# Evictions ahead of later weight splits, products between the pieces of a chain's front, and a second chain begun inside the first one's end

## The chip, the cores and the metric

The kernel runs on one core of one Trainium2 chip. The metric is the device time of one execution in microseconds (us); the time given is the median of three runs. Three engines matter here: PE (TensorE, the matrix products), ACT (ScalarE) and DVE (VectorE). POOL (GpSimd) does a few additions, and SP (SyncE) issues the loads of the weights.

## What is computed

Two blocks of two layers each work on 256 tokens of width 1024, all in fp32. The first block (attention, Fourier and pooling mixers, mixture of experts) is not touched by the chain edits. The second block is, per layer:

```python
h = h + HALF * _swiglu(_rmsnorm(h, ffn1_norm[l]), ffn1_w_in[l], ffn1_w_out[l])
xn = _rmsnorm(h, mix_norm[l])
z = xn @ w_in[l]
z_rw = z_rw + shift_mu[l] * (_time_shift(z_rw) - z_rw)
r, k, v, xw, xa, xg = _split_cols(z_rw, RW_SPLITS)
y_a = _rwkv7_mixer(r, k, v, xw, xa, xg, ...)
y_b = _mlstm_mixer(mq, mk, mv, mo, mi, mf, ...)
u = jax.nn.sigmoid(g_a) * (y_a @ br_a[l]) + jax.nn.sigmoid(g_b) * (y_b @ br_b[l])
h = h + u @ w_out[l]
h = h + HALF * _swiglu(_rmsnorm(h, ffn2_norm[l]), ffn2_w_in[l], ffn2_w_out[l])
```

In the RWKV mixer the decay is built from `tanh(xw)`, a small product and a sigmoid; `a` is a sigmoid of a small product; `xg` goes through a sigmoid; the decay's running sum goes through exponentials; `kk` is `k * k_k`, divided by its norm. The recurrences of both mixers are worked out in chunks by triangular products.

## The kernel before

**Weights.** All weights lie in one stream in the order of use. SP loads them as tiles of 1536 KB into a ring. Every block of 128 x 1024 weights is one **job** of the class `Dense` (from L440). Its weights are split into a high and a low half: ACT copies the high half (`zh`, L451), DVE subtracts (`zl`, L452). There are three pairs of such halves. The products then run on PE, and an **eviction** (a closure in `evq`) takes the result out of PSUM.

**The pump.** `pump(k)` runs the next k jobs. Ahead of job n it writes out the splits of all jobs up to n + 2, then the products of job n, then a hook if the job has one, then the evictions of the jobs before n. `need(n)` (called by `upto`) pumps to job n and writes out the evictions of all jobs below n. The order in the text is a priority: the framework's planner puts an instruction of later text ahead on its engine where the earlier one isn't ready by its reckoning, so an engine's queue need not follow the text. Once planned, each queue runs in order.

**The mixer phase** (`mixer`) has 47 jobs: 4 for the mLSTM values, 15 for the RWKV inputs (`zr_job`, L1480 on for its eviction; list `ZR`: the three small inputs, k, r, v), 12 for the other mLSTM inputs, 16 for the gates (`zg_job`, whose eviction is a sigmoid on ACT, L1556). Then come 8 `br` jobs, which need the outputs of both chains, and 8 `w2` jobs, which need the evictions of the `br` jobs.

**The chains.** `rwkv` and `mlstm` are generators: a list of steps with a `yield` between two, and after each step the loop at the end of the phase pumps one job. `rwkv` has 22 yields; `mlstm` has 7. `START2 = 22` starts `mlstm` after the 22nd step, that is, just before the last piece of `rwkv`. The **front** of `rwkv` (L1630 to L1680) is: tanh and two sigmoids of the small inputs (L1632 to L1634), 8 small products with 8 sigmoids (L1645), 4 scans (L1649), sums, four exponentials (L1660 to L1664), squares of k (L1668), copies of k with a scale (L1670), the norm (`rows8`). Calls of `upto(ZN + ...)` in it say which jobs must be through. The **end** of `rwkv` is the output y (copies L500, sums L503), its mean (a product with a constant, written `ps<-t,c`), squares L1899, norm, gate, and the split of y_a. The end of `mlstm` is its norm, L2039, and the split of y_b (ACT L1294, DVE L503, written `p<-t`), which the `br` jobs wait for.

The other phases, in order: first block (two layers), then per layer of the second block a feed-forward phase (`ffn_phase`, 44 + 24 jobs; two jobs share one eviction), the mixer phase, a second feed-forward phase.

Of the kernel before, what the change touches and what calls it, by code (L numbers as in the profile page):

```python
# [9 lines left out]
AF = mybir.ActivationFunctionType  # L10
# [8 lines left out]
LATE = 0  # L19
QKO = [4, 5, 0, 1, 2, 3]  # L20
NSLOT = 16
START2 = 22
TILE_W = 3072
FF = 2816
NFF = FF // 128
# [408 lines left out]
class Dense:  # L434
# [21 lines left out]
    def flush(self, upto=None):  # L456
        while self.evq and (upto is None or self.evq[0][0] < upto):
            self.evq.pop(0)[1]()

    def pump(self, k=None):  # L460
        stop = len(self.jobs) if k is None else min(len(self.jobs), self.n + k)
        while self.n < stop:
            while self.split_n < min(len(self.jobs), self.n + self.ahead + 1):
                self.do_split(self.split_n)
                self.split_n += 1
            key, mm, ev = self.jobs[self.n]
            pair = self.split.pop(self.n)
            mm(*pair)
            self.whl.put(pair)
            if self.n in self.hooks:  # L470
                self.hooks.pop(self.n)()
            if not self.hold:
                self.flush(self.n + 1 - self.lag)
            if ev is not None:
                self.evq.append((self.n, ev))
            self.n += 1
        if k is None:
            self.flush()

# [780 lines left out]
def second(env):  # L1260
# [29 lines left out]
    def v4(t):  # L1290
        return t.rearrange("p (a b) -> p a b", b=256)
# [142 lines left out]
    def mixer(l, after):  # L1434
# [32 lines left out]
        def zr_job(b):  # L1467
            box = {}

            def run(wh, wl):  # L1470
                box["p"] = PS.get()
                block(box["p"][:, 0:256], wh, wl, Q2)

            def ev():
                p = box["p"]
                if b < 4:
                    dst = r[:, b * 4:b * 4 + 4]
                elif b < 12:
                    dst = g3(v4((k, v)[b // 4 - 1])[:, b % 4])
                else:  # L1480
                    dst = g3(lo_[:, b - 12])
                z = zs.get()
                acopy(z[:, 3:259], p[:, 0:256])
                d = sm.get()
                A.activation(d[:, 0:256], p[:, 0:256], AF.Copy, scale=mu1[:, b:b + 1])
                PS.put(p)
                V.scalar_tensor_tensor(dst, g3(z[:, 2:258]), K["mu", l][:, b:b + 1], g3(d[:, 0:256]), op0=ALU.mult, op1=ALU.add)
                sm.put(d)
                zs.put(z)
            return (("zr", l, b), run, ev)  # L1490
# [77 lines left out]
        def upto(n):  # L1568
            dn.need(n0 + n)
# [28 lines left out]
        def g3(ap):  # L1598
            return ap.rearrange("p (n c) -> p n c", c=64)
# [29 lines left out]

        def rwkv():  # L1630
            upto(ZN + 3)
            A.activation(lo_[0:64, 0], lo_[0:64, 0], AF.Tanh)  # L1632
            A.activation(lo_[:, 1], lo_[:, 1], AF.Sigmoid)
            A.activation(lo_[0:32, 2], lo_[0:32, 2], AF.Sigmoid)  # L1634
            upto(ZN + 5)
            sig, a = S.get(), S.get()
            for (lo, hi, dst, bias) in ((0, 64, sig, "rw_w0"), (64, 128, a, "rw_a0")):
                for half in range(2):
                    p = PS.get()
                    for n in range(2):  # L1640
                        hp = half * 2 + n
                        mm(p[:, n * 256:n * 256 + 256], lw[lo:hi, hp * 128:hp * 128 + 128], lo_[lo:hi, 0])
                    for n in range(2):
                        hp = half * 2 + n
                        A.activation(v4(dst)[:, hp], p[:, n * 256:n * 256 + 256], AF.Sigmoid, bias=K[bias, l][:, hp:hp + 1])  # L1645
                    PS.put(p)
            cum = S.get()
            for hp in range(4):
                V.tensor_tensor_scan(v4(cum)[:, hp], C["scan"], v4(sig)[:, hp], 0.0, op0=ALU.mult, op1=ALU.add)  # L1649

            f = rcol.get()
            f3 = f[:, 0:16].rearrange("p (h c) -> p h c", c=4)
# [5 lines left out]
            tt(V, g3(cum), g3(cum), ctr.rearrange("p (n o) -> p n o", o=1).to_broadcast([128, 16, 64]), ALU.subtract)  # L1658
            tt(V, sig, cum, sig, ALU.subtract)
            A.activation(f3[:, :, 0:3], f3[:, :, 0:3], AF.Exp, scale=-cexp)  # L1660
            A.activation(sig, sig, AF.Exp, scale=-cexp)
            em = S.get()
            A.activation(em, cum, AF.Exp, scale=cexp)
            A.activation(cum, cum, AF.Exp, scale=-cexp)  # L1664
            upto(ZN + 7)
            t = S.get()
            for hp in range(4):
                A.activation(v4(t)[:, hp], v4(k)[:, hp], AF.Square, scale=K["rw_k_k", l][:, hp:hp + 1])  # L1668
            for hp in range(4):
                A.activation(kk[:, hp * 4:hp * 4 + 4], g3(v4(k)[:, hp]), AF.Copy, scale=K["rw_k_k", l][:, hp:hp + 1])  # L1670
            upto(ZN + 8)
            nrm = yield from rows8(t, None, None, 1e-24)
            for hf in range(2):
                c = slice(hf * 8, hf * 8 + 8)
# [86 lines left out]
            LT, QB = tri(bm)  # L1761
            yield
            AT, QK = tri(km)
            yield
            vtok = turn(v, v)
            yield
            Gm = S.get()
# [120 lines left out]
                        tt(V, yv, g3(b_[2][w]), yv, ALU.add)  # L1888
            PS.put(*b_)
            S.put(vtok, U, QK, QB, SS)  # L1890
            yield
            b_ = two_banks()
            for hp in range(4):
                mm(b_[hp // 2][:, (hp % 2) * 256:(hp % 2) * 256 + 256], C["bmean"], v4(y)[:, hp])
# [151 lines left out]
        n = 0  # L2046
        while alive:
            for g in list(alive):
                try:
                    next(g)  # L2050
                except StopIteration:
                    alive.remove(g)
                dn.pump(1)
                n += 1
                if n == START2:
                    alive.append(g2)
# [152 lines left out]
```

## Time and profile before

| what | value |
|---|---|
| median of 3 runs | 2723.25 us (2720.39 to 2723.99) |
| profiled execution, device time | 2721.18 us |
| its span in the trace | 2719.4 us |
| mean granted PE clock | 0.974 |
| PE busy, share of the span | 91% |
| first block | up to 1378 us |
| first mixer / second mixer, as read below | 1583.4 to 1841.4 us / 2240.5 to 2499 us |

PE is busy for nine tenths of the span, so the reader looks for the places where it isn't, and asks what it waited for there. The granted clock of PE is 1.00 at its full speed (2.4 GHz) and 0.50 at its lower one (1.2 GHz): a stretch with a mean of 0.77 has lost 0.23 of its length. The trace counts time from the start of the span.

### The profile page before, as it was taken

What the parts mean: (1) busy time and instruction counts of PE and PEld (TensorE: products, weight loads), DVE (VectorE), ACT (ScalarE), POOL (GpSimd) and SP (SyncE); (2) the same over time, 40 slices, a digit from 0 to 9 for tenths busy, and PEclk for the clock granted to TensorE, in tenths of its full rate; (3) what the DMA queues carried; (4) which work ended last, traced back from release to release, by engine and by line L of the source; (5) the groups of instructions that cost most, each with busy time, mean ns of one, the idle gap of its engine ahead of it and who ended that gap; (6) DMA issues with size and microseconds to landing.
All of it is one profiled execution on the core that took longest, in us unless ns stands there. A gap on an engine that the chain in (4) does not pass through costs nothing.

```text
span 2719.4 us, 39461 instructions
## 1 busy us (share of the span) xinstructions
PE 2463.7 (91%) x16536; PEld 1713.8 (63%) x16536; DVE 1249.3 (46%) x2221; ACT 952.9 (35%) x1620; POOL 157.5 (6%) x185
## 2 busy tenths in 40 slices
PE   7998999999999865656689999999999999999998
PEld 4756443333366511111158889898888889989887
DVE  3544221111265300000057668557667677756765
ACT  3332100000043200000045574446556557454654
POOL 0100000000010000000011100011111100001111
PEclk9999999999999899899989999999999999999999
DMA  8372799999946699999965533234545543223553
GB/s 342 117 297 103 333 395 425 426 426 426 426 195 264 266 426 426 425 426 426 426 259 193 186 140 118 95 121 175 196 180 189 196 181 140 95 94 118 186 183 111
DMA packets 66915, 689.95 MB, mean 254 GB/s; under 512 B 7216, under 2 KB 9648, under 8 KB 11056
## 3 DMA queue, kind: packets, MB, share of 16 engines
q1 hardware_dynamic: 65584, 681.76, 62.6%
q0 software_dynamic: 720, 4.76, 0.4%
q8 instruction: 129, 2.11, 0.3%
q10 hardware_dynamic: 432, 0.91, 0.1%
q14 instruction: 50, 0.41, 0.0%
HBM read 686.35 MB, written 1.05 MB: 253 GB/s over the span
## 4 chain that ended last, share of the span: by engine, by line
PE 73%; DMA 20%; DVE 4%; ACT 2%; issue 1%; POOL 0%; SPq 0%; DVEq 0%; ACTq 0%; POOLq 0%
PE ps L492 71%; DMA xring<-in_w_dram 9%; DMA ring<-in_w_dram 7%; DMA mring<-in_w_dram 4%; PE ps L1736 1%; DVE zl L452 1%; ACT zh L451 1%; DVE t L503 0%; PE ps L892 0%; POOL sm L503 0%; DMA h<-in_cT_dram 0%; DVE sm L503 0%; DVE hl L1038 0%; DVE p L1339 0%; DVE t L1649 0%
## 5 line engine op out<-in xcount | busy, mean ns | idle before, releaser
L452 DVE TENSOR_TENSOR zl<-ring,zh 128x1024 fp32r<-128x1024 f32 (+1 forms) x398 | 480.0, 1207 | 287.6 <-ACT zh L451 287.2
L451 ACT ACTIVATE zh<-ring 128x1024 fp32r<-128x1024 f32 (+1 forms) x398 | 414.3, 1041 | 485.5 <-PE ps L492 385.6
L492 PE MATMUL ps<-p,zh 128*128 128x512 f32 (+1 forms) x1664 | 542.6, 378 | 11.9 <-ACT zh L451 5.7
L492 PE MATMUL ps<-p,zl 128*128 128x256 f32 x1536 | 433.4, 282 | 1.8 <-DVE zl L452 1.8
L492 PEld LDWEIGHTS ps<-p,zh 128*128 128x128 f32 x1664 | 307.1, 190 | 71.9 <-ACT zh L451 6.6
L492 PE MATMUL ps<-xring,m 128*64 128x512 f32 (+1 forms) x1280 | 296.7, 616 | 57.6 <-DMA xring<-in_w_dram 56.8
L492 PE MATMUL ps<-ring,m 128*64 128x512 f32 (+1 forms) x1288 | 298.1, 611 | 48.7 <-DMA ring<-in_w_dram 48.1
L492 PE MATMUL ps<-q,zh 128*128 128x256 f32 x1632 | 316.1, 293 | 7.5 <-ACT q L1294 2.9
L492 PEld LDWEIGHTS ps<-p,zl 128*128 128x128 f32 x1536 | 293.5, 191 | 2.5 <-DVE zl L452 2.3
L492 PEld LDWEIGHTS ps<-q,zh 128*128 128x128 f32 x1632 | 260.7, 196 | 17.9 <-ACT q L1294 4.4
L492 PE MATMUL ps<-act,zh 128*128 128x512 f32 x704 | 247.6, 393 | 0.0
L492 PEld LDWEIGHTS ps<-xring,m 128*64 128x64 f32 (+1 forms) x1280 | 86.1, 127 | 246.6 <-issue 140.6
L492 PE MATMUL ps<-q,zl 128*128 128x256 f32 x816 | 235.4, 289 | 2.9 <-DVE zl L452 1.5
L492 PEld LDWEIGHTS ps<-ring,m 128*64 128x64 f32 (+1 forms) x1288 | 88.0, 127 | 229.9 <-issue 136.0
L503 DVE TENSOR_TENSOR m<-ps,m 128x512 f32<-128x512 f32 x24 | 16.6, 692 | 447.2 <-PE ps L492 447.2
L492 PE MATMUL ps<-act,zl 128*128 128x256 f32 x704 | 199.6, 284 | 0.0
L492 PEld LDWEIGHTS ps<-q,zl 128*128 128x128 f32 x816 | 160.2, 196 | 1.9 <-DVE zl L452 1.9
L500 ACT ACTIVATE m<-ps 128x512 f32<-128x512 f32 x24 | 14.3, 598 | 419.7 <-PE ps L1190 284.9
L1202 DVE SCALAR_TENSOR_TENSOR h<-ps,mods,h 128x256 f32<-128x256 f32 x160 | 69.5, 480 | 187.4 <-PE ps L492 187.4
L492 PEld LDWEIGHTS ps<-act,zh 128*128 128x128 f32 x704 | 132.2, 188 | 30.2
L492 PE MATMUL ps<-mring,m 128*32 128x512 f32 x504 | 91.5, 659 | 59.4 <-DMA mring<-in_w_dram 59.4
L492 PEld LDWEIGHTS ps<-act,zl 128*128 128x128 f32 x704 | 132.4, 188 | 0.0
(323 smaller groups left out, 3053.3 us busy)
## 6 DMA issues: line engine op xcount, KB each, us to landing
ring<-in_w_dram SPq DMA_DIRECT2D x228, 1536.0 KB, 8.2
xring<-in_w_dram SPq DMA_DIRECT2D x129, 1536.0 KB, 15.9
mring<-in_w_dram SPq DMA_DIRECT2D x42, 1536.0 KB, 29.4
ring<-in_w_dram SPq DMA_DIRECT2D x31, 1408.0 KB, 5.9
ring<-in_w_dram SPq DMA_DIRECT2D x4, 1280.0 KB, 19.5
lora<-in_lora_dram POOLq DMA_DIRECT2D x2, 768.0 KB, 7.3
cf<-in_cf_dram POOLq DMA_DIRECT2D x1, 1392.5 KB, 12.4
h<-in_xT_dram SPq DMA_DIRECT2D x1, 1024.0 KB, 6.3
```

The source lines that it names most:

```text
L451: nc.scalar.activation(hi[:, :c], w, AF.Copy)
L452: nc.vector.tensor_tensor(lo[:, :c], w, hi[:, :c].bitcast(F32), op=ALU.subtract)
L492: PE.matmul(o, lhsT=lhsT, rhs=rhs, start=start, stop=stop, skip_group_check=True)
L500: A.activation(o, a, AF.Copy)
L503: e.tensor_tensor(o, a, b, op=op)
L1202: V.scalar_tensor_tensor(h[:, kb, c], p[:, c], mods[i][:, 5, kb, r:r + 1], h[:, kb, c], op0=ALU.mult, op1=ALU.add)
L1736: PE.transpose(b_[n // 4][:, (n % 4) * 128:(n % 4) * 128 + 128], src[:, n * 128:n * 128 + 128], ident)
```

## The change

`pump` now writes out the splits only up to job n + 1 ahead of job n, and that of job n + 2 behind the hook and the evictions that follow job n (new method `split_to`). In the eviction of `zr_job` the plain copy moves from ACT to DVE. In the front of `rwkv` the two sigmoids stand ahead of the tanh; the 8 small products go to four banks at once; six `upto` calls are spread between the pieces (one more job is asked for by the time of the norm); the sigmoid of the running sum's exponential follows a job; the scaled copies of k move from ACT to DVE. After the third step of `rwkv` no job is pumped (`yield 0`), after the step that builds y two are (`yield 2`). `mlstm` starts after step 19 instead of 22, and as long as `rwkv` lives, a step of `mlstm` pumps nothing.

```diff
--- before.py
+++ after.py
@@ -19,7 +19,7 @@
 LATE = 0
 QKO = [4, 5, 0, 1, 2, 3]
 NSLOT = 16
-START2 = 22
+START2 = 19
 TILE_W = 3072
 FF = 2816
 NFF = FF // 128
@@ -457,12 +457,15 @@
         while self.evq and (upto is None or self.evq[0][0] < upto):
             self.evq.pop(0)[1]()
 
+    def split_to(self, n):
+        while self.split_n < min(len(self.jobs), n):
+            self.do_split(self.split_n)
+            self.split_n += 1
+
     def pump(self, k=None):
         stop = len(self.jobs) if k is None else min(len(self.jobs), self.n + k)
         while self.n < stop:
-            while self.split_n < min(len(self.jobs), self.n + self.ahead + 1):
-                self.do_split(self.split_n)
-                self.split_n += 1
+            self.split_to(self.n + self.ahead)
             key, mm, ev = self.jobs[self.n]
             pair = self.split.pop(self.n)
             mm(*pair)
@@ -474,6 +477,7 @@
             if ev is not None:
                 self.evq.append((self.n, ev))
             self.n += 1
+            self.split_to(self.n + self.ahead)
         if k is None:
             self.flush()
 
@@ -1480,7 +1484,7 @@
                 else:
                     dst = g3(lo_[:, b - 12])
                 z = zs.get()
-                acopy(z[:, 3:259], p[:, 0:256])
+                V.tensor_copy(z[:, 3:259], p[:, 0:256])
                 d = sm.get()
                 A.activation(d[:, 0:256], p[:, 0:256], AF.Copy, scale=mu1[:, b:b + 1])
                 PS.put(p)
@@ -1629,24 +1633,26 @@
 
         def rwkv():
             upto(ZN + 3)
-            A.activation(lo_[0:64, 0], lo_[0:64, 0], AF.Tanh)
             A.activation(lo_[:, 1], lo_[:, 1], AF.Sigmoid)
             A.activation(lo_[0:32, 2], lo_[0:32, 2], AF.Sigmoid)
-            upto(ZN + 5)
+            A.activation(lo_[0:64, 0], lo_[0:64, 0], AF.Tanh)
+            upto(ZN + 4)
             sig, a = S.get(), S.get()
-            for (lo, hi, dst, bias) in ((0, 64, sig, "rw_w0"), (64, 128, a, "rw_a0")):
-                for half in range(2):
-                    p = PS.get()
-                    for n in range(2):
-                        hp = half * 2 + n
-                        mm(p[:, n * 256:n * 256 + 256], lw[lo:hi, hp * 128:hp * 128 + 128], lo_[lo:hi, 0])
-                    for n in range(2):
-                        hp = half * 2 + n
-                        A.activation(v4(dst)[:, hp], p[:, n * 256:n * 256 + 256], AF.Sigmoid, bias=K[bias, l][:, hp:hp + 1])
-                    PS.put(p)
+            up = [[PS.get(), PS.get()] for _ in range(2)]
+            for hp in range(4):
+                for m, (lo, hi) in enumerate(((0, 64), (64, 128))):
+                    mm(up[m][hp // 2][:, (hp % 2) * 256:(hp % 2) * 256 + 256], lw[lo:hi, hp * 128:hp * 128 + 128], lo_[lo:hi, 0])
+            for m, (dst, bias) in enumerate(((sig, "rw_w0"), (a, "rw_a0"))):
+                if m:
+                    upto(ZN + 5)
+                for hp in range(4):
+                    A.activation(v4(dst)[:, hp], up[m][hp // 2][:, (hp % 2) * 256:(hp % 2) * 256 + 256], AF.Sigmoid,
+                                 bias=K[bias, l][:, hp:hp + 1])
+                PS.put(*up[m])
             cum = S.get()
             for hp in range(4):
                 V.tensor_tensor_scan(v4(cum)[:, hp], C["scan"], v4(sig)[:, hp], 0.0, op0=ALU.mult, op1=ALU.add)
+            upto(ZN + 6)
 
             f = rcol.get()
             f3 = f[:, 0:16].rearrange("p (h c) -> p h c", c=4)
@@ -1658,17 +1664,18 @@
             tt(V, g3(cum), g3(cum), ctr.rearrange("p (n o) -> p n o", o=1).to_broadcast([128, 16, 64]), ALU.subtract)
             tt(V, sig, cum, sig, ALU.subtract)
             A.activation(f3[:, :, 0:3], f3[:, :, 0:3], AF.Exp, scale=-cexp)
-            A.activation(sig, sig, AF.Exp, scale=-cexp)
             em = S.get()
             A.activation(em, cum, AF.Exp, scale=cexp)
+            upto(ZN + 7)
+            A.activation(sig, sig, AF.Exp, scale=-cexp)
             A.activation(cum, cum, AF.Exp, scale=-cexp)
-            upto(ZN + 7)
+            upto(ZN + 8)
             t = S.get()
             for hp in range(4):
                 A.activation(v4(t)[:, hp], v4(k)[:, hp], AF.Square, scale=K["rw_k_k", l][:, hp:hp + 1])
             for hp in range(4):
-                A.activation(kk[:, hp * 4:hp * 4 + 4], g3(v4(k)[:, hp]), AF.Copy, scale=K["rw_k_k", l][:, hp:hp + 1])
-            upto(ZN + 8)
+                V.tensor_scalar(kk[:, hp * 4:hp * 4 + 4], g3(v4(k)[:, hp]), K["rw_k_k", l][:, hp:hp + 1], None, op0=ALU.mult)
+            upto(ZN + 9)
             nrm = yield from rows8(t, None, None, 1e-24)
             for hf in range(2):
                 c = slice(hf * 8, hf * 8 + 8)
@@ -1761,7 +1768,7 @@
             LT, QB = tri(bm)
             yield
             AT, QK = tri(km)
-            yield
+            yield 0
             vtok = turn(v, v)
             yield
             Gm = S.get()
@@ -1888,7 +1895,7 @@
                         tt(V, yv, g3(b_[2][w]), yv, ALU.add)
             PS.put(*b_)
             S.put(vtok, U, QK, QB, SS)
-            yield
+            yield 2
             b_ = two_banks()
             for hp in range(4):
                 mm(b_[hp // 2][:, (hp % 2) * 256:(hp % 2) * 256 + 256], C["bmean"], v4(y)[:, hp])
@@ -2046,11 +2053,12 @@
         n = 0
         while alive:
             for g in list(alive):
+                k_ = None
                 try:
-                    next(g)
+                    k_ = next(g)
                 except StopIteration:
                     alive.remove(g)
-                dn.pump(1)
+                dn.pump(0 if g is g2 and g1 in alive else 1 if k_ is None else k_)
                 n += 1
                 if n == START2:
                     alive.append(g2)
```

## Rows read from the trace of the kernel before

**Rows 1.** The page's busy time of PE, its share of the span, its instructions.

```profile
PE 2463.7 (91%) x16536; PEld 1713.8 (63%) x16536; DVE 1249.3 (46%) x2221; ACT 952.9 (35%) x1620; POOL 157.5 (6%) x185
```

**Rows 2.** The chain that ended last, share of the span by engine.

```profile
PE 73%; DMA 20%; DVE 4%; ACT 2%; issue 1%; POOL 0%; SPq 0%; DVEq 0%; ACTq 0%; POOLq 0%
```

**Rows 3.** Windows (length, busy time by engine, clock, DMA): feed-forward, both mixers.

```profile
1400.00:1583.00 183.00, 183.00 (x1042) 160.33 (x1041) 127.84 (x191) 105.09 (x180) 22.43 (x28) 1.00 0.52 188
...
1583.40:1841.40 258.00, 247.84 (x2998) 232.53 (x2996) 170.50 (x291) 140.12 (x221) 8.69 (x7) 0.97 0.30 111
2240.50:2499.00 258.50, 248.46 (x3006) 233.58 (x3004) 173.29 (x292) 142.93 (x226) 8.11 (x6) 0.97 0.30 107
```

**Rows 4.** Windows again, order PE, PEld, DVE, ACT, POOL: the mixer's front.

```profile
1599.50:1617.20 17.70, 15.87 (x122) 14.88 (x120) 11.75 (x17) 15.85 (x32) 0.00 (x0) 1.00 0.25 90
...
1612.40:1627.40 15.00, 12.94 (x88) 12.32 (x89) 5.72 (x12) 14.00 (x26) 0.00 (x0) 0.77 0.28 106
1627.50:1655.50 28.00, 28.00 (x308) 26.14 (x305) 27.87 (x43) 10.77 (x19) 0.00 (x0) 1.00 0.32 114
...
2268.00:2288.00 20.00, 18.15 (x129) 17.56 (x128) 9.43 (x18) 16.05 (x28) 0.00 (x0) 0.74 0.30 108
```

**Rows 5.** ACT in order of time, front (start, us, line, operation, tiles, shapes).

```profile
1595.52 1.28 ACT L1632 ACT_TABLE_LOAD   x1
...
1597.88 1.28 ACT L1633 ACT_TABLE_LOAD   x1
...
1608.90 1.28 ACT L1660 ACT_TABLE_LOAD   x1
1610.20 0.21 ACT L1660 ACTIVATE rc<-rc 128x12 f32<-128x12 f32 x1
...
1613.19 1.04 ACT L1664 ACTIVATE t<-t 128x1024 f32<-128x1024 f32 x1
1614.14 1.04 ACT L451 ACTIVATE zh<-ring 128x1024 fp32r<-128x1024 f32 x1
```

**Rows 6.** DVE groups by form (count, us, ns): first mixer, then 1627.5 to 1655.5.

```profile
L503 DVE TENSOR_TENSOR t<-ps,c 128x256 f32<-128x256 f32 x16 | 5.6, 413 | 0.0
L1739 DVE COPY t<-ps 128x512 f32<-128x512 f32 x8 | 5.5, 684 | 0.8 <-PE ps L1736 0.8
...
L1487 DVE SCALAR_TENSOR_TENSOR t<-zs,k,sm 128x256 f32<-128x256 f32 x4 | 1.9, 479 | 0.1
```

**Rows 7.** PE in time at `ps<-t,c`; PE's waits, 2400 to 2430.

```profile
1753.58 0.67 PE L492 MATMUL ps<-t,c 128*128 128x256 f32 x2 [1.79 <-DVE t L503]
...
PE ps L492 <- issue: 1.4, 1, 1.4
PE ps L492 <- DVE t L503: 0.9, 1, 0.9
```

**Rows 8.** Windows: the chains' ends, one job, the wait ahead of `br` and `w2`.

```profile
1744.00:1783.00 39.00, 36.82 (x417) 32.43 (x416) 21.96 (x39) 29.28 (x40) 0.59 (x1) 0.96 0.28 103
...
1787.99:1790.94 2.95, 2.95 (x27) 2.95 (x26) 1.78 (x3) 0.23 (x1) 0.00 (x0) 1.00 0.97 412
...
1808.00:1822.00 14.00, 10.91 (x78) 10.50 (x77) 8.44 (x15) 4.41 (x6) 0.72 (x1) 0.88 0.01 1
...
1834.00:1842.00 8.00, 5.96 (x43) 5.15 (x43) 6.26 (x13) 3.30 (x6) 1.22 (x1) 1.00 0.38 152
```

**Rows 9.** Feed-forward: ACT and DVE in time, and the 88 evictions' silu group.

```profile
1451.60 1.06 ACT L451 ACTIVATE zh<-ring 128x1024 fp32r<-128x1024 f32 x1 [1.12 <-issue]
...
1455.35 0.40 ACT L1294 ACTIVATE act<-sm 128x256 fp32r<-128x256 f32 x1
...
1457.15 1.06 ACT L451 ACTIVATE zh<-ring 128x1024 fp32r<-128x1024 f32 x1 [1.14 <-PE ps L492]
...
1452.69 1.23 DVE L452 TENSOR_TENSOR zl<-ring,zh 128x1024 fp32r<-128x1024 f32 x1 [0.41 <-ACT zh L451]
...
L1392 ACT ACTIVATE sm<-sm 128x256 f32<-128x256 f32 x88 | 36.0, 409 | 5.4 <-DVE sm L503 5.3
```

## What the change should do, worked out from these rows

> **What bounds the kernel now.** I read the page's busy times first: PE works 91% of the span [rows 1]. The chain that ended last says the same from the other side: 73% of it is PE, 20% loads of weights, ACT and DVE have 6% [rows 2]. The loads belong to the first block, which the chain edits don't reach. So the next view is busy time by stretch, for the parts that the change touches. A feed-forward phase has PE at 183.00 of 183.00 us: nothing is to be had there [rows 3]. The two mixers have 247.84 of 258.00 and 248.46 of 258.50: 10.2 and 10.0 us of idle PE, plus a mean clock of 0.97, which is 0.03 x 258 = 8 us in each [rows 3]. The number of products doesn't change, so some 36 us is all that a new order can win in the mixers, and the question is which of those holes it closes. They are few. The front of `rwkv`: PE is idle 15.00 - 12.94 = 2.06 us, and the clock of that stretch is 0.77, so 15 x 0.23 = 3.5 us more; in the second mixer 20.00 - 18.15 = 1.85 us and 20 x 0.26 = 5.2 us [rows 4]. The end of `rwkv`: PE waits 1.79 us for y; in the second mixer 1.4 + 0.9 = 2.3 us [rows 7]. The end of `mlstm`: 14.00 - 10.91 = 3.09 us idle, clock 0.88, so 14 x 0.12 = 1.7 us more, and the second mixer repeats both. Ahead of the `w2` jobs: 8.00 - 5.96 = 2.04 us, repeated too [rows 8].
>
> **The front.** Between 1599.5 and 1617.2 ACT is busy 15.85 of 17.70 us, DVE 11.75 [rows 4]. In the queue the split of the next weights (`zh`, 1614.14) stands right behind the exponentials (L1664 at 1613.19) [rows 5], and PE ran dry meanwhile. The change does two things there. It asks for single jobs between the pieces, so a split comes up before the exponentials and not behind them all. And it takes work off ACT: per mixer 15 plain copies and 4 scaled ones go to DVE. A DVE instruction of 128 x 256 from PSUM takes 0.41 us, and a copy of 128 x 512 takes what a difference of that size does, 0.68 [rows 6], so I price each at 0.41. In the front's 17.7 us that is some 4 + 4 of them: 3.3 us, which makes DVE's 11.75 into 15.1 of 17.7. It still fits. I take the idle time as closed but for 0.4 us a mixer (3.1 of 3.9 won). The low clock began only after the idle time, and in the next 28 us, with PE at 28.00 of 28.00, it is 1.00 [rows 4]; so with the hole most of the loss should go: 4.9 of 8.7. Together **8.0 us**, with bounds 0 and 12.6.
>
> The tanh now stands behind the sigmoids. Today a table load of 1.28 us stands ahead of the tanh and another ahead of the sigmoid [rows 5]. Its input is the first of the three to be ready, so a queue set by readiness keeps tanh first and both loads; the other way one load fewer or one more is ACT's 1.28 us a mixer, inside the bounds above. I take nothing. The Trainium skill (ScalarE: Activation LUTs, "Table sets: the hidden batching unit") lists tanh in the set of the sigmoid as well as in that of exp; by it, sigmoid first would save one load, and the sum would gain at most 2.6 us in two mixers; today's order with its two loads agrees with it, and no row here shows the other order.
>
> **DVE after the front.** From 1627.5 to 1655.5 DVE is busy 27.87 of 28.00 us [rows 4]: it paces the chain there, under a PE that is just as full. Seven evictions of `zr` jobs fall in this stretch (4 in the row, 3 more of that form that write r) [rows 6]. Seven copies of 0.41 are 2.9 us a mixer, 5.7 in two, on the path if PE has no other job, nothing if it has. I take about half, **-2.4 us**; bounds 0 and -5.7.
>
> **The end of `rwkv`.** `yield 2` puts a second job of 2.95 us [rows 8] where PE now waits 1.79 us for y (2.3 in the second mixer) [rows 7]. Its weights can be split by then, since three pairs exist. The job was due after step 3 before, next to the stretch where PE is at 28.00 of 28.00 [rows 4]. I take **3.6** of 4.1 us; bounds 0 and 4.1.
>
> **The end of `mlstm`.** Steps 1 to 3 of `mlstm` now run inside the last three pieces of `rwkv` and pump nothing. So of the 47 jobs the last three are pumped later: one after step 7, one after the end of the chain, one by the final pump, where before none was left after step 6. Two jobs, 5.9 us, stand against a hole of 3.09 us [rows 8]. That closes it with room: I take 5.6 of 6.2 us idle and half of the clock's 3.4, **7.3 us**; bounds 0 and 9.6. The price is paid inside: the overlapped stretch has two jobs fewer to hide behind. From 1744 to 1783 ACT is busy 29.28 of 39.00 us [rows 8]; without 5.9 us of that time and without two splits of 1.06 it would have 27.2 of 33.1.
>
> **Evictions ahead of splits.** In the feed-forward phases, where 88 evictions lie [rows 9], the split that begins at 1451.60 is done at 1453.9 (DVE 1452.69 + 1.23); it is used two jobs after it became possible, when the split two jobs on begins, 1457.15: 3.2 us of slack hide the edit [rows 9]. If the whole eviction went ahead of it (its last ACT copy ends at 1455.75, less the 1.06 us of the split that no longer stands in its way), the split would be done at 1454.7 + 1.06 + 1.23 = 1457.0, still just in time. I take 0; bound: 0.1 us x 88 = -9 us. Loads of weights that SP issues when a split is through move by the same fraction of a microsecond, in phases where the loads aren't late. Ahead of `w2` the evictions of the last `br` jobs come earlier, by at most the 2.04 us twice; I take **0.4 us**, bounds 0 and 4.1.
>
> **The sum.** 8.0 - 2.4 + 3.6 + 7.3 + 0.4 = 16.9 us. The profiled execution took 2721.18 us, 2 us below the median; there the sum gives 2704, and against the median 2723.25 it gives **2706 us**. All upper bounds together are 30.4 us, 2693.
>
> **Rivals.**
> (A) The front stays as it is, because DVE takes over as the bound: 15.1 of 17.7 us plus waits leaves little room, and the copies cost their full 5.7 - 0.9 us. Against it: DVE has 5.95 us free there today [rows 4]. Then 3.6 + 7.3 + 0.4 - 4.8 = 6.5 us: **2717**.
> (B) The change doesn't do what it says. Queues follow readiness and not the text, as the split copy of the eviction behind a later job's split in rows 9 shows (1455.35), and the overlap only shifts the holes: **2722**. Against it: the number of jobs after each step is fixed by data and banks, not by readiness.
> (C) Slower: table loads. In the overlap the gate evictions (sigmoid) meet exp, ln, square root of two chains instead of one, and each change of function set costs ACT a load of 1.28 us, after which it goes on at once (1608.90 + 1.28 to 1610.20) [rows 5]. ACT has 33.1 - 27.2 = 5.9 us free there, so it decides from five more loads a mixer on. With ten more, 12.8 us, ACT overruns by 6.9 us a mixer and the end's gains are lost: 13.8 - 8.0 + 2.4 = 8 us slower, **2731**. For it: today the stretch already alternates. Against it: fewer jobs in it mean fewer gate evictions. The Trainium skill (ScalarE: Activation LUTs, "What ACT_TABLE_LOAD costs") puts a change of set at about 2.66 us, the load and a drain as long again; the row here shows 1.28 and no drain. By the page three more loads would already decide, and ten would give some 2759.
>
> **How the numbers follow.** A measurement of this kernel can tell about 0.2%, 5.4 us. Forecast 0.62, A 0.20, B 0.09, C 0.09. A lies close to that limit, so I count 0.12 of it as faster and 0.08 as the same: faster 0.74, same 0.17, slower 0.09. The range runs from all upper bounds, 2692, to 2722, which takes in A and half of B; C is left out.
>
> **What would show it.** In the front: a `zh` of L451 between the sigmoids L1645 and the exponentials, idle PE under 1 us, clock near 1.00 over 15 us. At `ps<-t,c`: 48 products ahead of it, no wait. At the end: `q` jobs between the norm of `mlstm` and the `br` jobs, no wait of 2.5 us for the split of y_b. DVE's full stretch: its length against 28 us. Wrong would be: a PE wait for `zl` instead of `zh` in the front (A), the same holes at later places (B), over ten loads of tables at the ends (C), or idle PE in the feed-forward phases.

## The result, and the profile after

The changed kernel takes 2691.70 us (median; 2689.02 to 2692.10) where the kernel before, timed beside it, takes 2721.82. The ratio is 0.9888, with a 95% interval of 0.9871 to 0.9905: 30.5 us less, 25.9 to 35.1. The forecast was 2706 in 2692 to 2722: right in sign and in the places, too small by nearly half, and the median lies just below the low end of the range. The profiled execution has a span of 2689.8 us. After the change, the lines of the code lie 4 to 7 further down: L492 is now L496, L503 is L507, L1294 is L1298.

First the windows that answer [rows 3, 4, 8]. Columns: window, its length, then busy us (and instructions) of PE, PEld, DVE, ACT, POOL, then the clock, the DMA share, GB/s.

```profile
1400.00:1583.00 183.00, 183.00 (x1046) 160.49 (x1045) 127.74 (x190) 105.37 (x181) 22.38 (x28) 1.00 0.51 186
1588.00:1848.00 260.00, 258.03 (x3145) 245.13 (x3146) 191.67 (x326) 144.06 (x219) 10.50 (x13) 0.99 0.33 121
2245.60:2505.60 260.00, 258.03 (x3126) 244.14 (x3125) 191.64 (x322) 144.15 (x220) 11.75 (x14) 0.99 0.32 118
1604.00:1622.00 18.00, 17.60 (x148) 17.40 (x148) 16.10 (x30) 15.50 (x26) 0.00 (x0) 1.00 0.38 146
1632.00:1660.00 28.00, 27.57 (x455) 25.19 (x455) 27.13 (x51) 9.75 (x17) 0.00 (x0) 1.00 0.31 114
2273.00:2293.00 20.00, 20.00 (x214) 18.21 (x213) 19.57 (x29) 9.62 (x15) 0.00 (x0) 1.00 0.41 159
1755.50:1762.50 7.00, 7.00 (x33) 6.83 (x33) 1.58 (x4) 4.55 (x7) 0.00 (x0) 0.52 0.01 2
1802.00:1826.00 24.00, 24.00 (x203) 24.00 (x202) 21.77 (x33) 12.15 (x17) 4.42 (x6) 1.00 0.54 198
1825.00:1849.00 24.00, 24.00 (x200) 23.95 (x199) 19.94 (x29) 14.26 (x24) 6.11 (x6) 1.00 0.50 171
```

The feed-forward phase is full as before. A stretch of 260 us in each mixer has 2.0 us of idle PE where there were 10, at a clock of 0.99 where there was 0.97. The front has no low clock left. The `br` jobs (from 1802) and the `w2` jobs (from 1825) run with no gap at all; before, there were holes of 3.09 and 2.04 us there [rows 8].

What PE still waits for in the first mixer (1588 to 1848), the longest of six entries (columns: engine, tile and line, waited for, us in total, times, longest):

```profile
PE ps L496 <- ACT sm L1489: 0.4, 1, 0.4
...
```

Before, the same list (1583.4 to 1841.4) began with the split of y_b and with y:

```profile
PE ps L492 <- ACT p L1294: 2.5, 1, 2.5
PE ps L492 <- DVE t L503: 1.8, 1, 1.8
...
```

To see where the 30 us came from I cut each mixer at products that both traces have: the first product of the RWKV inputs, the first of the chain's levels (`ps<-kr,t`), the first of the `br` jobs, the first and the last of the `w2` jobs. In the first mixer before, they start at 1586.88, 1638.70, 1805.42, 1835.39 and 1861.39. Lengths in us, first / second mixer:

| stage | before | after | saved in both |
|---|---|---|---|
| front: inputs to levels | 51.82 / 52.69 | 46.43 / 46.41 | 11.7 |
| middle: levels to first `br` product | 166.71 / 166.71 | 167.68 / 168.10 | -2.4 |
| `br` jobs | 29.98 / 29.97 | 23.04 / 23.04 | 13.9 |
| `w2` jobs | 26.00 / 26.93 | 22.95 / 22.96 | 7.0 |

Together 30.2 us. The norm of `mlstm` (16 products `ps<-common,rc`, 1.95 us from 1808.97 on before) moved from the third stage into the second; put back, the middle gained 1.5 and the end of `mlstm` 10.0. A stage read from one profile carries some 2 us of chance: with the old front, the second mixer has much the same idle PE there in three traces (1.85 to 2.07 us), but 10.24 us of low clock follow it in the kernel before, 6.83 in the run `t_only` and 3.41 in the run `t_yield`, both below.

### The profile page after: what moved, and what is told of

Its sections match the earlier page's. It is cut to its first block, busy times and chain, and to the rows that moved or that the text cites. A ratio compares the mean times of both kernels' runs of the same rounds, so it can differ in the third digit from the quotient of the medians.

```text
span 2689.8 us, 39423 instructions
## 1 busy us (share of the span) xinstructions
PE 2448.2 (91%) x16536; PEld 1704.7 (63%) x16536; DVE 1265.1 (47%) x2259; ACT 940.2 (35%) x1580; POOL 150.5 (6%) x185
## 4 chain that ended last, share of the span: by engine, by line
PE 75%; DMA 18%; DVE 4%; ACT 2%; issue 1%; SPq 0%; DVEq 0%; ACTq 0%
PE ps L496 74%; DMA xring<-in_w_dram 7%; DMA ring<-in_w_dram 7%; DMA mring<-in_w_dram 4%; DVE zl L452 1%; PE ps L1743 1%; DVE t L507 1%; ACT zh L451 0%; PE ps L896 0%; DMA h<-in_cT_dram 0%; DVE m L507 0%; DVE hl L1042 0%; PE ps L1194 0%; DVE p L1343 0%; DVE t L1654 0%
## 5 line engine op out<-in xcount | busy, mean ns | idle before, releaser
L496 PE MATMUL ps<-p,zh 128*128 128x512 f32 (+1 forms) x1664 | 538.6, 377 | 5.7 <-ACT zh L451 5.7
L496 PE MATMUL ps<-p,zl 128*128 128x256 f32 x1536 | 431.7, 281 | 1.8 <-DVE zl L452 1.8
L496 PE MATMUL ps<-xring,m 128*64 128x512 f32 (+1 forms) x1280 | 297.0, 616 | 58.6 <-DMA xring<-in_w_dram 57.6
L496 PEld LDWEIGHTS ps<-p,zh 128*128 128x128 f32 x1664 | 304.6, 189 | 64.9 <-ACT zh L451 6.6
L496 PE MATMUL ps<-ring,m 128*64 128x512 f32 (+1 forms) x1288 | 294.5, 602 | 49.4 <-DMA ring<-in_w_dram 48.9
L496 PE MATMUL ps<-q,zh 128*128 128x256 f32 x1632 | 310.0, 290 | 1.4 <-ACT q L1298 0.8
L496 PEld LDWEIGHTS ps<-p,zl 128*128 128x128 f32 x1536 | 291.9, 190 | 2.5 <-DVE zl L452 2.3
L496 PEld LDWEIGHTS ps<-q,zh 128*128 128x128 f32 x1632 | 257.2, 194 | 7.2 <-issue 1.8
L496 PE MATMUL ps<-act,zh 128*128 128x512 f32 x704 | 247.6, 394 | 0.0
L496 PEld LDWEIGHTS ps<-xring,m 128*64 128x64 f32 (+1 forms) x1280 | 86.7, 128 | 246.7 <-issue 139.7
L496 PE MATMUL ps<-q,zl 128*128 128x256 f32 x816 | 234.1, 288 | 0.8 <-DVE zl L452 0.8
L496 PEld LDWEIGHTS ps<-ring,m 128*64 128x64 f32 (+1 forms) x1288 | 88.2, 126 | 227.3 <-issue 134.1
L507 DVE TENSOR_TENSOR m<-ps,m 128x512 f32<-128x512 f32 x24 | 16.6, 691 | 447.6 <-PE ps L496 447.6
L496 PE MATMUL ps<-act,zl 128*128 128x256 f32 x704 | 199.6, 284 | 0.0
L496 PEld LDWEIGHTS ps<-q,zl 128*128 128x128 f32 x816 | 157.7, 193 | 2.3 <-DVE zl L452 1.2
L496 PEld LDWEIGHTS ps<-act,zh 128*128 128x128 f32 x704 | 132.2, 188 | 30.2
L496 PE MATMUL ps<-mring,m 128*32 128x512 f32 x504 | 92.4, 664 | 60.3 <-DMA mring<-in_w_dram 60.3
L496 PEld LDWEIGHTS ps<-act,zl 128*128 128x128 f32 x704 | 132.4, 188 | 0.0
```

The costliest lines, as they stand in the source:

```text
L496: PE.matmul(o, lhsT=lhsT, rhs=rhs, start=start, stop=stop, skip_group_check=True)
L507: e.tensor_tensor(o, a, b, op=op)
```

## Experiments

Differences in us below are the ratio's, times 2720; "gain" is against the kernel before.

**The parts, one at a time.** First the new order of splits and evictions alone:

```diff
...
-            while self.split_n < min(len(self.jobs), self.n + self.ahead + 1):
-                self.do_split(self.split_n)
-                self.split_n += 1
+            self.split_to(self.n + self.ahead)
...
             self.n += 1
+            self.split_to(self.n + self.ahead)
```

> The kernel before with one edit: the new order in pump (split of job n + 2 behind the evictions that follow job n). Theory 1 (the order of evictions and splits is worth more than the 0.4 us of the prediction): the stretch of the w2 jobs, 1835.4 to 1861.7 us before, shrinks by about 3 us in each mixer, the time falls by 5 to 7 us, to about 2716; the waits at the front, at y and at the end of mlstm stay at 2.1, 1.8 and 3.1 us. Rival (the w2 stretch shrank because the br jobs no longer start in halves ahead of y_b): no change, 2721 to 2723, PE idle of 2 us ahead of w2 stays.

Measured: 1.0009 (0.9999 to 1.0018). No gain is to be seen, and the stage of the `w2` jobs is 28.29 / 27.09 us, no shorter than before (the profile is of the longest of its ten runs). The order of the evictions doesn't close the hole ahead of `w2`.

The front alone (all hunks of the diff from L1480 to L1680):

> The kernel before with the edits of the front alone (order of the pieces, copies on DVE). Theory 1 (idle PE plus the low clock that follows it, nothing else): the 2.06 and 1.85 us of idle PE and the 3.5 and 5.2 us of clock go, 11 to 13 us faster, about 2710; the w2 stretch and the ends stay. Rival A of the prediction (DVE becomes the bound): 0 to 4 us faster.

Measured: 0.9961 (0.9947 to 0.9975), a gain of 10.6 us (7 to 14). The front is 46.40 / 46.42 us, as in the whole change; the `br` and `w2` stages stay as they were (29.98, 25.99).

The start of `mlstm`, the two yields and the loop's rule alone:

```diff
-START2 = 22
+START2 = 19
...
-            yield
+            yield 0
...
-            yield
+            yield 2
...
-                dn.pump(1)
+                dn.pump(0 if g is g2 and g1 in alive else 1 if k_ is None else k_)
```

> The kernel before with the later part alone (start of mlstm after step 19, yield 0 and yield 2, no pumping by mlstm while rwkv lives). Theory 1: the waits for y (1.8 and 2.3 us) and for y_b (2 x 3.1 us) go and the clock's 2 x 1.7 us at the end of mlstm with them: 11 to 14 us faster, about 2709. Rival C of the prediction (table loads in the overlap): more loads than before's at the ends, 0 to 8 us slower.

Measured: 0.9928 (0.9913 to 0.9943), 19.6 us. `br` takes 23.04 and `w2` 22.95 in both mixers: this part closes the hole ahead of `w2`, for which I had given it nothing. With the front's 10.6 it makes 30.2, the whole result.

The whole change without the new order of splits:

> The changed kernel with the old order in pump put back. Theory 1: the w2 stretch is 26 us again in each mixer and the time 5 to 7 us above the changed kernel, about 2698. Rival (halves of br jobs): as the changed kernel, 2691 to 2692, w2 stretch 23 us.

Measured: 0.9891 (0.9876 to 0.9906), against 0.9888 for the whole. In this company, too, the order makes no difference that the intervals can show.

**What the hole ahead of `w2` is.** The `br` jobs' evictions are sums: DVE multiplies twice (`sm<-ps,t`), POOL adds for the first six jobs, ACT and DVE split the sum (`q`). POOL in time, before (start, us, engine, line, operation, tiles, shapes, idle time ahead):

```profile
1818.71 0.72 POOL L503 TENSOR_TENSOR sm<-sm 128x256 f32<-128x256 f32 x1 [48.03 <-DVE sm L503]
1822.89 1.65 POOL L503 TENSOR_TENSOR sm<-sm 128x256 f32<-128x256 f32 x1 [3.45 <-DVE sm L503]
1826.19 1.65 POOL L503 TENSOR_TENSOR sm<-sm 128x256 f32<-128x256 f32 x1 [1.66 <-DVE sm L503]
```

and after:

```profile
1806.27 0.73 POOL L507 TENSOR_TENSOR sm<-sm 128x256 f32<-128x256 f32 x1 [35.08 <-DVE sm L507]
1809.16 0.74 POOL L507 TENSOR_TENSOR sm<-sm 128x256 f32<-128x256 f32 x1 [2.16 <-DVE sm L507]
```

The same addition takes 0.74 or 1.65 us. DVE beside it, before:

```profile
1818.80 1.72 DVE L452 TENSOR_TENSOR zl<-ring,zh 128x1024 fp32r<-128x1024 f32 x1 [0.18 <-ACT zh L451]
...
1822.73 1.21 DVE L452 TENSOR_TENSOR zl<-ring,zh 128x1024 fp32r<-128x1024 f32 x1
1825.02 0.43 DVE L503 TENSOR_TENSOR q<-sm,q 128x256 fp32r<-128x256 f32 x1 [1.08 <-ACT q L1294]
1825.37 0.75 DVE L503 TENSOR_TENSOR sm<-ps,t 128x256 f32<-128x256 f32 x2
1826.03 1.22 DVE L452 TENSOR_TENSOR zl<-ring,zh 128x1024 fp32r<-128x1024 f32 x1
```

and after:

```profile
1806.39 1.69 DVE L452 TENSOR_TENSOR zl<-ring,zh 128x1024 fp32r<-128x1024 f32 x1 [0.22 <-ACT zh L451]
```

Whichever of the two starts second is the one that gets longer. At 1818.71 POOL starts 0.09 us ahead of `zl` and takes 0.72, `zl` 1.72; at 1822.89 it starts 0.16 behind and takes 1.65, `zl` 1.21. The Trainium skill (SBUF — State Buffer, "SBUF: two separate sides") says that a DVE instruction with two SBUF inputs and a GpSimd instruction that reads SBUF share a port pair which the first to start holds to its end; these rows agree in kind (by the rule the second addition takes what is left of 1.21 plus 0.74, an estimate of some 1.8, where 1.65 is measured).

The price falls on a loop. ACT before, in the same stretch:

```profile
1824.57 0.42 ACT L1294 ACTIVATE q<-sm 128x256 fp32r<-128x256 f32 x1 [2.38 <-POOL sm L503]
1824.89 1.04 ACT L451 ACTIVATE zh<-ring 128x1024 fp32r<-128x1024 f32 x1
...
```

ACT's copy `q` waits for POOL. DVE's half of that split (1825.02) waits for the copy, the next multiplications (1825.37) stand behind it in DVE's queue, and POOL's next addition waits for them. `zh` has followed `q` on ACT meanwhile, so `zl` starts right behind the multiplications, 0.16 us ahead of POOL, and the addition is slow again. One turn is 1826.19 - 1822.89 = 3.30 us, and a `br` job takes PE 2.88 (23.04 for eight). So evictions that are late can't catch up, and where they start in time they fall back by 0.4 us a job; the first `w2` jobs, which need them all, pay it at once. Here the first addition starts 0.9 us behind the end of its job's products, the third 5.0 and the sixth 3.8: three jobs that end within 3.3 us bring most of the delay, and the slow turn keeps it. After the change POOL starts first; one turn is 2.90 us, close to PE's 2.88. The next run has DVE do all eight additions:

```diff
-                tt(G if b < 6 else V, t[:, 0:256], t[:, 0:256], t[:, 256:512], ALU.add)
+                tt(V, t[:, 0:256], t[:, 0:256], t[:, 256:512], ALU.add)
```

> The kernel before, with the addition in the evictions of the br jobs on DVE for all eight instead of on POOL for six. Theory 2 (each POOL addition of 0.74 us lasts 1.65 us because it stands against DVE's split of 1.23 us, and the loop ACT split - DVE - POOL then turns in 3.31 us where a job takes 2.9 us, so the evictions fall behind PE by 3 us until w2): the w2 stretch falls from 26.0 and 26.9 to about 23 us in each mixer, the time by 5 to 7 us, to about 2716; the waits for y_b stay. Rival (the w2 hole comes from the splits, three at once after the halves of br jobs): DVE has more to do, nothing gained, w2 stretch 26 us or more.

Measured: 0.9979 (0.9970 to 0.9988), 5.7 us. The `w2` stage is 22.92 us in both mixers by this edit alone. Its windows, over the same stretches as [rows 8]:

```profile
1834.00:1842.00 8.00, 8.00 (x69) 8.00 (x68) 7.56 (x15) 3.70 (x6) 0.00 (x0) 1.00 0.46 184
1808.00:1822.00 14.00, 10.91 (x79) 10.50 (x79) 8.28 (x21) 5.04 (x6) 0.00 (x0) 0.89 0.17 70
```

PE has 8.00 of 8.00 us at `w2`, while the wait for y_b, 10.91 of 14.00, is untouched. The hole was POOL's late addition: the three jobs still end close together here, and it is gone.

Why does an earlier `mlstm` get the fast order? In the kernel before, PE takes the y_a halves of three `br` jobs while it waits for y_b; then these three end close together and their splits crowd. If those halves are the cause, taking the y_b halves first should remove the hole:

```diff
-                for m in range(2):
+                for m in (1, 0):
...
-                            m == 0 and kb == 0, kb == 3)
+                            m == 1 and kb == 0, kb == 3)
```

> The kernel before, with the two halves of a br job exchanged: the half that needs y_b first, so no br job can start ahead of y_b. Theory 3 (the w2 hole is set off by the three half jobs ahead of y_b, which then end within 4.4 us and free three pairs at once): PE waits 4.3 us longer for y_b, about 7 us in each mixer, but the jobs then run whole and the w2 stretch is 23 us; the time is 1 to 3 us above before's in all. Rival (the hole comes with every series of br jobs on POOL): the longer wait for y_b and a w2 stretch of 26 us, 8 to 10 us slower than before.

Measured: 1.0024 (1.0014 to 1.0034), 6.5 us slower, since nothing runs ahead of y_b now; `w2` is 24.71 / 24.24 us, about half-way between 26.00 / 26.93 and 22.95. POOL in time:

```profile
1826.45 0.74 POOL L503 TENSOR_TENSOR sm<-sm 128x256 f32<-128x256 f32 x1 [2.16 <-DVE sm L503]
1829.36 1.72 POOL L503 TENSOR_TENSOR sm<-sm 128x256 f32<-128x256 f32 x1 [2.16 <-DVE sm L503]
...
```

Two additions go fast and then it tips into the slow order all the same. So the halves hasten the slow order but aren't needed for it. DVE beside these additions shows what tips it:

```profile
1826.51 1.77 DVE L452 TENSOR_TENSOR zl<-ring,zh 128x1024 fp32r<-128x1024 f32 x1
...
1829.25 1.23 DVE L452 TENSOR_TENSOR zl<-ring,zh 128x1024 fp32r<-128x1024 f32 x1
```

POOL's head start over `zl` is 0.06 us at the second addition, and at the third `zl` is 0.11 ahead: the splits come 2.74 us apart, the additions 2.91. In the changed kernel the head start shrinks too, since a turn of 2.90 us is a little longer than PE's 2.88. It is 0.12 us at the first addition (1806.27 against 1806.39), and at the sixth and last of them:

```profile
1820.76 0.74 POOL L507 TENSOR_TENSOR sm<-sm 128x256 f32<-128x256 f32 x1 [2.16 <-DVE sm L507]
...
1820.79 1.78 DVE L452 TENSOR_TENSOR zl<-ring,zh 128x1024 fp32r<-128x1024 f32 x1
```

So the fast order outlasts the six additions with 0.03 us of head start left. An earlier `mlstm` lets the `br` jobs come at an even pace, on which the head start lasts that long; it doesn't make the fast order safe. How it goes with more additions on POOL was not run.

**The start and the yields apart.** The start alone, with the loop's rule:

```diff
-START2 = 22
+START2 = 19
...
-                dn.pump(1)
+                dn.pump(0 if g is g2 and g1 in alive else 1 if k_ is None else k_)
```

> The kernel before with mlstm started after step 19 and without pumping by mlstm while rwkv lives, but with the old yields (one job after step 3 and one after y). Theory: this alone closes the hole ahead of y_b and with it the w2 hole, 2 x (3.1 + 1.7 + 3) = 15 to 16 us, about 2706; the wait for y stays at 1.8 and 2.3 us or moves. Rival (yield 2 is what closes the end): 0 to 5 us faster.

Measured: 0.9939 (0.9924 to 0.9953), 16.6 us. Windows at its `br` and `w2` jobs:

```profile
1804.00:1818.00 14.00, 14.00 (x119) 14.00 (x118) 12.22 (x16) 7.73 (x11) 2.21 (x3) 1.00 0.43 150
1826.00:1834.00 8.00, 8.00 (x69) 8.00 (x68) 6.67 (x14) 4.11 (x7) 0.00 (x0) 1.00 0.49 184
```

Both holes are gone by the start alone. The wait for y is gone too in the first mixer; in the second 1.3 us of 2.3 is left.

The two yields without the early start, again with the loop's rule:

```diff
-            yield
+            yield 0
...
-            yield
+            yield 2
...
-                dn.pump(1)
+                dn.pump(0 if g is g2 and g1 in alive else 1 if k_ is None else k_)
```

> The kernel before with yield 0 and yield 2 and the new pumping, but mlstm still started after step 22. Theory: the wait for y goes (4 us in both mixers), the holes ahead of y_b and w2 stay, 3 to 4 us faster, about 2717. Rival (the later steps also move the br jobs): over 8 us faster.

Measured: 0.9980 (0.9970 to 0.9991), 5.4 us (2 to 8). By stages (the profile is of its shortest run, 2711.71 us) the middle is 163.57 / 166.01 us, 3.8 less in both together, and `br` and `w2` stay at 29.99 and 26:

```profile
1808.00:1822.00 14.00, 11.55 (x81) 11.35 (x82) 8.88 (x15) 5.85 (x7) 2.46 (x3) 0.88 0.22 74
1834.00:1842.00 8.00, 6.13 (x46) 5.73 (x47) 6.20 (x12) 4.34 (x8) 0.05 (x1) 1.00 0.53 186
```

**The front's two halves.** The order and the `upto` calls without the copies, that is, without these lines of the diff (and without the last `upto` call's extra job):

```diff
-                acopy(z[:, 3:259], p[:, 0:256])
+                V.tensor_copy(z[:, 3:259], p[:, 0:256])
...
-                A.activation(kk[:, hp * 4:hp * 4 + 4], g3(v4(k)[:, hp]), AF.Copy, scale=K["rw_k_k", l][:, hp:hp + 1])
+                V.tensor_scalar(kk[:, hp * 4:hp * 4 + 4], g3(v4(k)[:, hp]), K["rw_k_k", l][:, hp:hp + 1], None, op0=ALU.mult)
```

> The kernel before with the new order in the front of rwkv, but the plain copies of the zr evictions and the scaled copies of k still on ACT. Theory (single jobs between the pieces let the splits come up before the exponentials): most of the front's gain, 6 to 9 us, about 2714, clock 1.00 over the front. Rival (ACT's load is what counts, so the moves to DVE bring the gain): 0 to 3 us, PE still idle over 1.5 us there.

Measured: 0.9991 (0.9981 to 1.0000), 2.4 us (0 to 5). Windows as in [rows 4]:

```profile
1599.50:1617.20 17.70, 15.32 (x127) 14.62 (x124) 13.61 (x19) 17.68 (x36) 0.00 (x0) 1.00 0.45 159
1612.40:1627.40 15.00, 12.88 (x99) 12.49 (x98) 5.94 (x13) 11.51 (x22) 0.00 (x0) 0.77 0.30 106
2268.00:2288.00 20.00, 17.87 (x140) 17.48 (x139) 10.67 (x17) 14.71 (x28) 0.00 (x0) 0.83 0.39 154
```

With the copies still on ACT, ACT is full, 17.68 of 17.70 us, and PE is idle as long as before. The reverse, those lines alone (with the one `upto` call behind them):

> The kernel before with the plain copies of the zr evictions and the scaled copies of k on DVE, in the old order of the front. Theory 4 (ACT's load sets the front; the new order alone gave 2 us): most of the front's 9 to 12 us, 6 to 9 us faster, about 2712. Rival (moves and order need each other, since the split still stands behind the exponentials): 1 to 4 us faster, PE still idle 1 us or more ahead of a split in the front.

Measured: 0.9974 (0.9962 to 0.9985), 7.1 us (4 to 10).

```profile
1599.50:1617.20 17.70, 16.14 (x123) 15.04 (x122) 13.33 (x24) 15.43 (x27) 0.00 (x0) 1.00 0.29 104
1612.40:1627.40 15.00, 13.44 (x126) 12.71 (x125) 11.92 (x23) 11.56 (x19) 0.00 (x0) 1.00 0.57 211
2268.00:2288.00 20.00, 19.25 (x162) 18.73 (x161) 16.78 (x32) 12.12 (x19) 0.00 (x0) 0.91 0.22 79
```

Of the 2.06 us of idle PE in the first mixer's front 1.56 are left (of 15.00), and the clock, 0.77 before, stays at 1.00 there. The move carries most of the front's gain. That the order needs the room on ACT to close the rest is read from the windows; by time the two parts alone add up to 9.5 us of the 10.6 that they gain together, which is no difference.

**A version beyond both.** What stands out next in the trace after is the begin of the second block: PE waits 5.54 and 0.15 us for `zh`, then 1.81 for `zl`, 7.50 in all, and runs at half clock for 10.24 us from 1383.67. The text scales the input first; here the first two splits are written ahead of it:

```diff
+        if pre is not None:
+            dn.split_to(dn.n + 2)
+            pre()
+            rms = stats.pop()
+        begin(rms)
...
-    for kb in range(8):
-        first(kb)
+    def prep_first():
+        for kb in range(8):
+            first(kb)
```

> The changed kernel with one step more: the first two splits of the second block's first phase are written ahead of the scaling of its inputs instead of behind it (only the first feed-forward phase). PE waits there 5.5 us for the first high half and 1.8 us for the first low half. Theory (a place in the queue, not data, holds the split): PE starts 3 to 4 us earlier, 2 to 4 us faster than the changed kernel, about 2688. Rival (the inputs' scaling on DVE, eight of 0.75 us, paces the first products anyway): 0 to 1 us.

Measured: 0.9881 (0.9867 to 0.9896), 2688.24 us, the lowest median here. Its PE in time shows what is left of the waits, 4.42 us for 7.50:

```profile
1380.49 0.50 PE L496 MATMUL ps<-p,zh 128*128 128x512 f32 x1 [2.45 <-ACT zh L451]
1381.43 0.50 PE L496 MATMUL ps<-p,zh 128*128 128x512 f32 x1 [0.44 <-ACT zh L451]
1383.42 0.58 PE L496 MATMUL ps<-p,zl 128*128 128x256 f32 x1 [1.24 <-DVE zl L452]
1384.29 0.79 PE L496 MATMUL ps<-p,zh 128*128 128x512 f32 x1 [0.29 <-DVE p L1343]
```

The low clock lasts 6.83 us there. That is 3.1 us of waits and 1.7 of clock; the two medians differ by 3.5, but the intervals of the two ratios overlap, so by time alone this step isn't proven.

## Why the prediction fell short

**The front (8.0, less 2.4 on DVE; came to 11.7 by stages, 10.6 timed).** The idle time went as forecast: 0.40 us is left in 1604 to 1622. The mechanism in the queue is there too, though the split stands between the exponentials and not ahead of the first: it comes just ahead of the one (L1670, of the tile `sig`, an exponential and no sigmoid) that the change puts behind a job. ACT in time, after:

```profile
1595.96 1.28 ACT L1638 ACT_TABLE_LOAD   x1
...
1599.68 1.28 ACT L1636 ACT_TABLE_LOAD   x1
...
1606.32 1.28 ACT L1666 ACT_TABLE_LOAD   x1
1607.61 0.21 ACT L1666 ACTIVATE rc<-rc 128x12 f32<-128x12 f32 x1
1608.63 1.06 ACT L1668 ACTIVATE t<-t 128x1024 f32<-128x1024 f32 x1 [0.81 <-DVE t L507]
1609.60 1.04 ACT L451 ACTIVATE zh<-ring 128x1024 fp32r<-128x1024 f32 x1
...
1610.89 1.05 ACT L1670 ACTIVATE t<-t 128x1024 f32<-128x1024 f32 x1
1611.85 1.04 ACT L451 ACTIVATE zh<-ring 128x1024 fp32r<-128x1024 f32 x1
```

Two terms were mis-sized. I took 4.9 of 8.7 us of clock; all of it came back, 1.00 in both fronts. And I took 2.4 us for DVE; it is full as forecast, 27.13 of 28.00, but PE loses only 0.43 there, since it has jobs to run beside. That is 3.8 and some 1.6 us, nearly the whole of the difference. How much clock there was to win is partly luck, since in other traces the second front's low clock is shorter by up to 6.83 us. The tanh went as forecast: the queue put it first all the same, and both loads stay, so the other order was never put to the test. Rival A, DVE as the front's bound, is out; so is C: the middles have 12 and 13 loads of tables both before and after, and ACT has 82.41 us of work in the first (81.68 before).

**The end of `rwkv` (3.6).** The wait is gone. PE in time, after: 48 products from 1741.27 on, then `t,c` with no idle time ahead of it.

```profile
1741.27 0.50 PE L496 MATMUL ps<-q,zh 128*128 128x256 f32 x2
...
1747.56 1.99 PE L496 MATMUL ps<-t,c 128*128 128x256 f32 x8
...
1752.35 1.99 PE L496 MATMUL ps<-t,common 4*128 4x256 f32 x8
1754.27 2.27 PE L496 MATMUL ps<-c,t 128*128 128x2 f32 x16
```

The yields alone are worth 3.8 us by stages, where I said 3.6, though the early start alone removes most of this wait as well. In the whole change the middle kept only 1.5, since more low clock came in that I hadn't counted: 6.83 us of it from 1755.72 in the first mixer, with no idle PE ahead of it, where before had 3.41 (from 1778.35), and 3.41 in the second, where before had none. Of these 6.83 us more, half, 3.4 us, is lost, which is more than enough for the difference.

**The end of `mlstm` (7.3; came to 10.0).** Right in mechanism: 43 recorded products of jobs run between the norm and the first `br` product (1797.10 to 1802.34), and the start alone does it. I took half of the clock's 3.4 us and 5.6 of the 6.2 idle; both came back whole, and a little more.

**Ahead of `w2` (0.4; came to 7.0).** This is the step that failed. I tied the hole to the order of evictions and splits, which is worth nothing, and gave it the bound 4.1 from one window of 2.04 us, when the stage is 3.05 and 3.97 us longer than eight jobs without a gap (in the second mixer 3.41 us of low clock follow the hole, from 2498.57). The cause was a loop over ACT, DVE and POOL with a turn of 3.30 us under a PE that needs one of 2.88, and the rows hinted at it: POOL's one addition takes 0.72 us in the window of the `br` jobs, and 1.22 us of another lie in that of `w2` [rows 8]. I priced POOL nowhere.

**Evictions ahead of splits (0).** Right as far as the intervals show: no gain alone, none with the rest. Rival B had a point in the tanh, where the queue did not follow the text; but the holes went and didn't come back at later places.

**The sum.** The range ended where all upper bounds meet, and the measured time lies just beyond. It was not reached as the sum had it. The front came near its bound (11.7 of 12.6), the end of `mlstm` and the `w2` jobs passed theirs (10.0 over 9.6, 7.0 over 4.1), and the middle stayed below (1.5 of 4.1); that this comes so close to the 30.4 of all upper bounds is chance. The terms aren't independent: the clock losses in the front and at y_b followed an idle PE that the change removed, and the early start removed two holes at once.

## What to carry to other kernels

Ahead of a stage that needs all results of the one before it, work out the turn of the loop that the evictions make through the engines' queues, and set it against PE's time for a job: a loop that is 0.4 us slower shows as one hole at the end, far from its cause. Where the loop's pace hangs on which of two engines starts first, look at how that head start changes from turn to turn: here it shrinks even in the good order. An operation whose duration differs between two windows of one trace is a row to follow up, even on an engine that is 6% busy. And when an idle PE goes, count the low clock that followed it as going with it, but look for stretches of small products elsewhere that may fall to the low clock without any idle time.

## What the hardware showed

An addition of 128 x 256 on POOL takes 0.74 us when it starts first, and 1.65 when it starts 0.16 us behind a DVE subtraction of 128 x 1024 with both inputs in SBUF; that subtraction takes 1.22 us alone and 1.69 to 1.78 behind POOL's addition. Whichever is second, it ends some 0.14 us sooner than if it had stood still until the first was through: 1.21 - 0.16 + 0.74 = 1.79 for the 1.65, and 0.73 - 0.12 + 1.22 = 1.83 for the 1.69.

Beside the low clock that follows an idle time (0.77 over 15 us in the front before), the granted clock fell to 0.52 over 7 us, its lower level, with PE busy throughout: what ran just before were 8 products of 4 x 256 and 16 of 128 x 2. Whether these small products are the reason wasn't tried. A load of ACT's function table is 1.28 us, and the next instruction starts 0.01 us after it (1606.32 and 1607.61).
